# One decoder layer on one core: the sample's value products written to two halves of the PE array, the first chunk in two transfers, and two groups of splits issued earlier

## The chip, the core and the metric

The kernel runs on one core of one Trainium2 chip. The metric is the device time of one execution in microseconds (us), lower is better. The time before is 885.13 us, the median of three executions (884.75 to 885.17). One further execution was recorded by the hardware profiler, and all rows quoted below come from that one.

Names used throughout: PE is TensorE (PEld its weight loads, LDWEIGHTS), DVE is VectorE, ACT is ScalarE, POOL is GpSimd, and SP is the engine that issues most of the DMA transfers. Where an engine's name ends in q, its instruction sequencer is meant.

## The reference

One layer of a decoder is computed for two groups of requests that share the weights: a prompt of 512 tokens, and a sample of 8 requests with 8 new tokens each (64 tokens). The model width is 1024.

```
h   = x @ w_in                      # u | v | q | k | values | gate_A | gate_B
u   = gelu(h_u);  v = layer_norm(gelu(h_v))
y_a = u * (tril(W_s[g]) @ v_chunk + b_s[g])          # 8 groups, chunks of 128 tokens
y_b = attention(q, k, values)       # 16 heads on 4 key/value heads, window 128, sinks, relative bias
m   = (sigmoid(gate_A) * (y_a @ w_pa) + sigmoid(gate_B) * (y_b @ w_pb)) @ w_o
x   = layer_norm(alpha * x + m)
x   = layer_norm(alpha * x + (silu(x @ w_gate) * (x @ w_up)) @ w_down)
```

For the sample, each of the 8 requests attends to 128 cached keys and values and to its own new ones. The outputs are both groups' rows, the updated windows of keys and values, and the normalised v rows of the sample.

## The kernel before

**Precision and splits.** All large products are made in float32 quality from two pieces per operand: `split` (L116) copies a source to a "hi" tile in the fp32r type on ACT (L117) and puts source minus hi in a "lo" tile on DVE (L118). A product is three matmuls: hi by hi, hi by lo, lo by hi (`product` L287, `fm` L300, `tm` L313). Weights arrive as units of 128x1024 in a ring of three raw buffers, and hi and lo live in rings of four each. So a weight unit is fetched by SP, split on ACT and DVE, and read by PE, each some units ahead of the next.

**Order.** The kernel is written against a framework that records the instructions and orders them per engine; where the code says `manual_schedule`, the order is the order in which the code calls them. Every engine runs its own instructions in that order, and semaphores tie the engines together.

**Opening (L400 to L438).** The first products (key tile 0 and query tile 0) run over the 8 chunks of the model width. A chunk holds 576 token columns (512 + 64) and 256 weight columns in one tile, `open{k}`. Chunk 0 comes in three transfers (288 token columns, 256 weight columns, 288 token columns), each other chunk in one of 832 columns. For each chunk ACT and DVE split the tokens into X and the weights into hi and lo, and PE runs 12 matmuls of 288 columns into `ps`. Ahead of that `warm_up` (L392) runs six matmuls of zeros.

**Sample's value products (L733, `sample_values`).** The probabilities of the sample lie transposed in `spT` (cached keys, 128 rows) and `spN` (new keys, 64 rows). For each of the 4 key/value heads g there is one matmul with the new values as weights (64 rows, 64 columns, 256 moving columns) and 8 matmuls, one per request, with the cached values `vc` as weights (128 rows, 64 columns, 32 moving columns). They are in plain float32, and each is two PE instructions in the trace. The result `pso` stands in partitions 0 to 63 of a PSUM bank, for g = 0 and 2 in columns 0 to 255 and for g = 1 and 3 in columns 256 to 511. These 36 matmuls stand between the first and the second weight unit of the first half of the v projection (`acc_v`, L915 to L921).

**Pairs (L216, `pair`).** Two output tiles that share their activations are made with seven half products instead of eight, Strassen-like, of 12 matmuls each. Their weights are B11, B21, B22 and combinations T1 to T4 of them. PE's order in a pair is B11, T1, (the T4 of the pair before), T2, B22, B21, T3. The weights are split in groups: B11 and T1 from buffer a, "B22, B21" from buffer b, "T3, T2" from buffer t (step "2" of `weight_group`, L199), T4 last. `plan` says ahead of which half product each split is called, and `spots` names the places in a pair at which one piece of waiting work (`todo`) is called (`spare`, L211).

**Gates and merge (L997).** Seven pairs make the remaining gates (i = 0 to 6, tiles `xg, yg, zg`). Their `todo` list holds 17 pieces: 5 steps of the last normalisations, the 8 spatial gates, and 4 of the splits of the gated inputs `yA0` to `yA3`; a pair takes two, at its places 0 and 6, and what is left over is called after the last pair (L1034). Then come the products with w_pa (`pspa`, 48 matmuls each, 5 of them in a row), and then four pairs with w_pb (`xp, yp, zp`), each of the first three followed by one more `pspa` product. In the loop over these pairs (L1086) the split "T3, T2" of pair i was called at place 0 of pair i, that is after `end_pairs` and `times` of pair i-1: these two put on DVE the last multiplications of the pair before (L1092) and those of the `pspa` product (L1064).

Of the kernel before, what the change touches and what calls it, by code (L numbers as in the profile page):

```python
# [18 lines left out]
P = 128  # L19
D = 1024  # L20
KC = D // P
NP = 512
NS = 64
NT = NP + NS
HB = NT // 2
NB = NP // P
H = 16
HD = 64
# [51 lines left out]
class Builder:  # L80
# [284 lines left out]
    def build(self):  # L365
        psum = lambda name, bufs: self.tc.tile_pool(
            name=name, bufs=bufs, space=bass.MemoryType.PSUM, reuse_waits="tile")
        with psum("pp0", 3) as self.pp, psum("pb0", 2) as self.pb:
            self.constants()
            self.projections_and_attention()  # L370
        with psum("pb", 8) as self.pb:
            self.sample_first()
            self.gmlp()
            self.merge()
            self.output_projection()
            self.ffn()
            self.ffn_down()
# [22 lines left out]
    def load_x(self):  # L400
        nc = self.nc
        self.open = [self.C([NT + 256], F32, f"open{k}") for k in range(KC)]
        self.open_w = [self.phi.tile([P, 1024], F32R, tag="hi", name=f"hi{i}") for i in range(2)], [
            self.plo.tile([P, 1024], F32R, tag="lo", name=f"lo{i}") for i in range(2)]
        for k, t in enumerate(self.open):
            for s in (slice(0, HB), slice(NT, NT + 256), slice(HB, NT)) if k == 0 else (slice(0, NT + 256),):
                nc.sync.dma_start(out=t[:, s], in_=self.I["open"][:, k, s])
            if k == 3:
                self.bias_lookup()
        self.fetch(2)  # L410

    def opening_chunk(self, k, tiles):

        src = self.open[k]
        w = slice(256 * (k % 4), 256 * (k % 4) + 256)
        wh, wl = (t[k // 4][:, w] for t in self.open_w)
        tokens = lambda t0, t1: self.split(
            self.X[:, k, t0:t1], self.X[:, k, NT + t0 : NT + t1], src[:, t0:t1])
        if k:
            tokens(0, NT)  # L420
        else:
            tokens(0, HB)
        self.split(wh, wl, src[:, NT:])
        if k == 0:
            tokens(HB, NT)
        if k == 5:
            self.bias_copies()
        xh, xl = self.xact(k)
        for b in range(2):
            s = slice(b * HB, (b + 1) * HB)  # L430
            for c in range(2):
                o = tiles[c][:, b, :HB]
                cols = slice(P * c, P * c + P)
                self.mm(o, wh[:, cols], xh[:, s], k == 0, False)
                self.mm(o, wh[:, cols], xl[:, s], False, False)
                self.mm(o, wl[:, cols], xh[:, s], False, k == KC - 1)
        if k == 3:
            self.bias_products()  # L438
# [294 lines left out]
    def sample_values(self, vc, pT, pN):  # L733
        nc = self.nc
        po = [self.bank(f"pso{c}") for c in range(2)]
        outs = [po[g // 2][:HD, 256 * (g % 2) : 256 * (g % 2) + 256].rearrange("p (b q) -> p b q", b=DB)
                for g in range(G)]
        for g, o in enumerate(outs):
            self.mm(o, self.avS[:NS, HD * g : HD * g + HD], pN[:NS, :, 32 * g : 32 * g + 32], True, False)
            for b in range(DB):  # L740
                self.mm(o[:, b], vc[b // 4][:, b % 4, HD * g : HD * g + HD], pT[:, b, 32 * g : 32 * g + 32],
                        False, b == DB - 1)
        for g, o in enumerate(outs):
            for r in range(4):
                i = r % 2
# [7 lines left out]
    def projections_and_attention(self):  # L753
# [4 lines left out]
        self.kraw = misc[:, :384].rearrange("p (c t) -> p c t", c=2)  # L758
        self.Z = self.C([G, 4, 32], F32, "Z")
        self.kt, self.qs, self.u, self.T = [], {}, [], []  # L760
        self.warm_up()
        tiles = [self.PS(f"ps0_{c}") for c in range(2)]
        with self.tc.manual_schedule():
            self.load_x()
# [232 lines left out]
    def merge(self):  # L997
# [27 lines left out]
        with self.tc.manual_schedule():  # L1025
            for i in range(7):
                if i in (3, 4):
                    g, u = (self.SG(f"gb{i}_{k}") for k in range(2))
                else:
                    t = self.C([2, NT], F32, f"T{i}")  # L1030
                    g, u = t[:, 0], t[:, 1]
                (T if i < 3 else gB).extend((g, u))
                gates(i, g, u, i < 6)
        for w in self.todo:  # L1034
            w()
# [50 lines left out]
        def pairs(i):  # L1086
# [27 lines left out]
            else:  # L1114
                late, last = one, one
            stacks = (stack,) if i else ()
            plan = {0: (w["2"],) if i else (), 2: (one,), 3: (w["4"],), 6: (late,) + stacks, 7: (last,) + stacks}
            self.pair(f"p{i}", left, g, u, lambda: mul(ga[:, lo], g[:, lo], ga[:, lo]), final, plan=plan)
            if follows:
                self.w = nxt[0]  # L1120
                f = lambda t: t.rearrange("p (a b) -> p a b", a=KC)
                ps = product(plain + i, tuple(f(t) for t in self.pieces[n]))
                self.end_pairs()
                times(plain + i, ps)

# [311 lines left out]
def _opening(x, w_in):  # L1437

    w = np.concatenate([w_in[:, 3072 : 3072 + P], w_in[:, 2048 : 2048 + P]], 1)
    return np.concatenate([x.T, w], 1).reshape(KC, P, NT + 256).transpose(1, 0, 2)  # L1440


_OUTS = {
# [56 lines left out]
```

## Time and profile before

| What | Value |
|---|---|
| Median of three executions | 885.13 us |
| Profiled execution, its own time | 885.03 us |
| Span from its first to its last instruction | 883.3 us |
| PE busy in the span | 872.7 us (99%) |
| DVE, ACT, POOL busy | 630.2 us, 406.2 us, 193.9 us |
| Mean granted TensorE clock | 0.997 |
| Sample's value products on PE | from 192.03 to 198.51 us |

In a row of the timeline the first number is the start in us from the span's start and the second the duration in us of all instructions that the row merges; then come the engine, the source line, the operation, the names of what is written and read with its shape, and the count. In square brackets stands how long the engine sat idle before, and what ended that. Matmuls are pipelined: each is recorded as longer than the distance to the next, so distances between starts tell the pace.

### The profile page before, as it was taken

What the parts mean: (1) busy time and instruction counts of PE and PEld (TensorE: products, weight loads), DVE (VectorE), ACT (ScalarE), POOL (GpSimd) and SP (SyncE); (2) the same over time, 40 slices, a digit from 0 to 9 for tenths busy, and PEclk for the clock granted to TensorE, in tenths of its full rate; (3) what the DMA queues carried; (4) which work ended last, traced back from release to release, by engine and by line L of the source; (5) the groups of instructions that cost most, each with busy time, mean ns of one, the idle gap of its engine ahead of it and who ended that gap; (6) DMA issues with size and microseconds to landing.
All of it is one profiled execution on the core that took longest, in us unless ns stands there. A gap on an engine that the chain in (4) does not pass through costs nothing.

```text
span 883.3 us, 14728 instructions
## 1 busy us (share of the span) xinstructions
PE 872.7 (99%) x5907; PEld 820.6 (93%) x5907; DVE 630.2 (71%) x933; ACT 406.2 (46%) x770; POOL 193.9 (22%) x205
## 2 busy tenths in 40 slices
PE   9999999999999999999999999999999999999996
PEld 7999999988899999999888999999999998888885
DVE  5878897646789779767768777777777789224237
ACT  6566666565364456233522544444444457111110
POOL 1013324241342113033302222222222210000003
PEclk9999999999999999999999999999999999999998
DMA  8422125145023224324550022322333235222202
GB/s 303 153 99 72 50 72 163 45 170 162 29 104 102 75 93 144 135 78 159 179 187 14 1 72 96 96 96 96 96 97 96 96 96 191 96 72 96 72 1 107
DMA packets 31312, 91.85 MB, mean 104 GB/s; under 512 B 3979, under 2 KB 9516, under 8 KB 31212
## 3 DMA queue, kind: packets, MB, share of 16 engines
q1 hardware_dynamic: 30908, 88.64, 30.1%
q10 hardware_dynamic: 336, 2.28, 0.7%
q8 instruction: 46, 0.75, 0.4%
q14 instruction: 22, 0.18, 0.1%
HBM read 86.77 MB, written 6.10 MB: 105 GB/s over the span
## 4 chain that ended last, share of the span: by engine, by line
PE 93%; DVE 4%; ACT 1%; issue 1%; DMA 0%; POOL 0%; SPq 0%; DVEq 0%; ACTq 0%; POOLq 0%
PE d L298 16%; PE xf L298 14%; PE zf L298 7%; PE acc_v L298 6%; PE acc_o L298 6%; PE pspa L298 6%; PE xg L298 5%; PE psu L298 5%; PE yf L298 4%; PE psq L298 4%; PE ffn L298 3%; PE zg L298 3%; PE xp L298 2%; PE psav L298 2%; PE psg L298 1%; PE ps L298 1%
## 5 line engine op out<-in xcount | busy, mean ns | idle before, releaser
L118 DVE TENSOR_TENSOR lo<-raw,hi 128x1024 fp32r<-128x1024 f32 x70 | 86.2, 1239 | 93.4 <-ACT hi L117 93.0
L118 DVE TENSOR_TENSOR glo<-raw,ghi 128x1024 fp32r<-128x1024 f32 (+1 forms) x93 | 100.8, 1087 | 55.1 <-ACT ghi L117 55.1
L298 PE MATMUL d<-hi,h 128*128 128x512 f32 (+1 forms) x440 | 128.0, 368 | 0.0
L117 ACT CAST hi<-raw 128x1024 fp32r<-128x1024 f32 x70 | 72.7, 1049 | 103.2 <-PE d L298 82.6
L117 ACT CAST ghi<-raw 128x1024 fp32r<-128x1024 f32 (+1 forms) x93 | 83.4, 900 | 59.1 <-DVE raw L180 54.5
L298 PEld LDWEIGHTS d<-hi,h 128*128 128x128 f32 x440 | 79.8, 188 | 13.8
L298 PE MATMUL d<-lo,h 128*128 128x512 f32 (+1 forms) x242 | 89.6, 370 | 0.0
L180 POOL TENSOR_TENSOR raw<-raw,t 128x512 f32<-128x512 f32 x31 | 40.7, 1314 | 197.8 <-DVE glo L118 151.4
L180 POOL TENSOR_TENSOR t<-raw,raw 128x512 f32<-128x512 f32 x31 | 42.2, 1361 | 118.5 <-DVE raw L180 118.5
L298 PE MATMUL xf<-x1T,ghi 128*128 128x288 f32 x320 | 65.0, 295 | 0.0
L118 DVE TENSOR_TENSOR glo<-t,ghi 128x1024 fp32r<-128x1024 f32 x31 | 64.5, 2082 | 0.0
L298 PEld LDWEIGHTS d<-lo,h 128*128 128x128 f32 x242 | 45.6, 188 | 7.8
L298 PEld LDWEIGHTS xf<-x1T,ghi 128*128 128x128 f32 x320 | 51.4, 188 | 0.3 <-DVE u L229 0.2
L328 POOL TENSOR_SCALAR lnr<-lnmv 128x1 f32<-128x1 f32 (+1 forms) x15 | 13.2, 883 | 168.1 <-DVE lnmv L346 164.8
L642 POOL TENSOR_SCALAR_AFFINE_SELECT pc<-pt 128x512 fp32r<-128x512 f32 x24 | 23.2, 968 | 113.4 <-ACT pt L117 111.7
L298 PE MATMUL xf<-x1T,glo 128*128 128x288 f32 x160 | 47.1, 294 | 0.0
L298 PE MATMUL acc_o<-hi,m 128*128 128x512 f32 x144 | 46.3, 391 | 0.0
L298 PE MATMUL pspa<-yA,hi 128*128 128x288 f32 x256 | 44.6, 294 | 0.3 <-DVE yA L118 0.3
L618 ACT ACTIVATE work<-work,att 128x128 f32<-128x128 f32 x64 | 25.0, 392 | 42.1 <-DVE att L615 37.6
L298 PE MATMUL psu<-X,hi 128*128 128x288 f32 x256 | 44.1, 294 | 0.0
L298 PE MATMUL acc_v<-hi,X 128*128 128x512 f32 x128 | 41.6, 391 | 0.0
L298 PE MATMUL psq<-X,hi 128*128 128x288 f32 x224 | 38.8, 294 | 0.3 <-DVE kt L510 0.3
(369 smaller groups left out, 2479.6 us busy)
## 6 DMA issues: line engine op xcount, KB each, us to landing
raw<-in_wall_dram SPq DMA_DIRECT2D x132, 512.0 KB
open<-in_open_dram SPq DMA_DIRECT2D x7, 416.0 KB
xr<-in_xT_dram SPq DMA_DIRECT2D x8, 288.0 KB
z<-in_xtok_dram SPq DMA_DIRECT2D x4, 512.0 KB
out_y_prompt_dram<-z SPq DMA_DIRECT2D x3, 512.0 KB
circ<-bout SPq DMA_DIRECT2D x1, 1024.0 KB
Bsel<-circ SPq DMA_DIRECT2D x2, 512.0 KB
kc<-in_kcT_dram SPq DMA_DIRECT2D x2, 512.0 KB
```

The costliest lines, as they stand in the source:

```text
L117: self.nc.scalar.copy(out=hi, in_=src)
L118: return self.nc.vector.tensor_tensor(out=lo, in0=src, in1=hi.bitcast(F32), op=ALU.subtract)
L180: sub = lambda e, out, x, y: e.tensor_tensor(out=out, in0=x, in1=y, op=ALU.subtract)
L298: self.last_mm = self.nc.tensor.matmul(out, l, r, start=start, stop=stop, **more)
L328: self.nc.gpsimd.tensor_scalar_add(r[:n], mv[:n, 1:2], EPS)
L618: nc.scalar.activation(out=pr[:, r], in_=sel[:, r], func=AF.Exp, bias=nm[:, r : r + 1], accum_out=rs[:, r : r + 1])
L642: self.selected = nc.gpsimd.affine_select(out=f(out[:, i]), in_=f(pt[:, i].bitcast(F32)), pattern=[[0, 4], [sign, P]], compare_op=cmp, fil ...
```

## The change

There are four edits.

1. `sample_values`: key/value heads 1 and 3 now write partitions 64 to 127 of their bank, columns 0 to 255, where heads 0 and 2 write partitions 0 to 63. All four matmuls with the new values come first; then, for each bank, the matmuls of its two heads alternate request by request.
2. Opening: the host puts the weight columns ahead of the token columns in each chunk. Chunk 0 comes in two transfers, of 544 columns (weights and the first 288 tokens) and of 288. `warm_up` is called ahead of `constants`.
3. Pairs with w_pb: step "2" (T3, T2) of the next pair is called right after the `pspa` product and ahead of `end_pairs`.
4. Last pair of the gates (i = 6): `spots` becomes (0, 4, 5, 6), so four pieces of `todo` are called within it.

```diff
         with psum("pp0", 3) as self.pp, psum("pb0", 2) as self.pb:
+            self.warm_up()
             self.constants()
...
-            for s in (slice(0, HB), slice(NT, NT + 256), slice(HB, NT)) if k == 0 else (slice(0, NT + 256),):
+            for s in (slice(0, 256 + HB), slice(256 + HB, 256 + NT)) if k == 0 else (slice(0, 256 + NT),):
                 nc.sync.dma_start(out=t[:, s], in_=self.I["open"][:, k, s])
...
-        src = self.open[k]
+        first, src = self.open[k][:, :256], self.open[k][:, 256:]
...
-        self.split(wh, wl, src[:, NT:])
+        self.split(wh, wl, first)
...
-        outs = [po[g // 2][:HD, 256 * (g % 2) : 256 * (g % 2) + 256].rearrange("p (b q) -> p b q", b=DB)
+        outs = [po[g // 2][HD * (g % 2) : HD * (g % 2) + HD, :256].rearrange("p (b q) -> p b q", b=DB)
                 for g in range(G)]
+        hd, q = (lambda g: slice(HD * g, HD * g + HD)), (lambda g: slice(32 * g, 32 * g + 32))
         for g, o in enumerate(outs):
-            self.mm(o, self.avS[:NS, HD * g : HD * g + HD], pN[:NS, :, 32 * g : 32 * g + 32], True, False)
+            self.mm(o, self.avS[:NS, hd(g)], pN[:NS, :, q(g)], True, False)
+        for c in range(2):
             for b in range(DB):
-                self.mm(o[:, b], vc[b // 4][:, b % 4, HD * g : HD * g + HD], pT[:, b, 32 * g : 32 * g + 32],
-                        False, b == DB - 1)
+                for g in (2 * c, 2 * c + 1):
+                    self.mm(outs[g][:, b], vc[b // 4][:, b % 4, hd(g)], pT[:, b, q(g)],
+                            False, b == DB - 1)
...
-        self.warm_up()
         tiles = [self.PS(f"ps0_{c}") for c in range(2)]
...
                 (T if i < 3 else gB).extend((g, u))
+                if i == 6:
+                    self.spots = (0, 4, 5, 6)
                 gates(i, g, u, i < 6)
...
-            plan = {0: (w["2"],) if i else (), 2: (one,), 3: (w["4"],), 6: (late,) + stacks, 7: (last,) + stacks}
+            plan = {2: (one,), 3: (w["4"],), 6: (late,) + stacks, 7: (last,) + stacks}
...
                 ps = product(plain + i, tuple(f(t) for t in self.pieces[n]))
+                self.w["2"]()
                 self.end_pairs()
                 times(plain + i, ps)
...
-    return np.concatenate([x.T, w], 1).reshape(KC, P, NT + 256).transpose(1, 0, 2)
+    return np.concatenate([w, x.T], 1).reshape(KC, P, NT + 256).transpose(1, 0, 2)
```

How the order of instructions moves is shown at three places; x4 behind a row counts equal instructions that follow each other.

PE at the sample's value products, before (pso0 and pso1 are the two PSUM banks, vc0 and vc1 the cached values of requests 0 to 3 and 4 to 7, misc holds the new values; heads 0 and 1 go to pso0, heads 2 and 3 to pso1):

```order
L298 MATMUL acc_v0_4_2424<-lo22_2237,XS_102 128x512
L298 MATMUL pso0_2459<-spN_2393,misc_103 64x256
L298 MATMUL pso0_2459<-spT_2383,vc0_1972 64x32 x4
L298 MATMUL pso0_2459<-spT_2383,vc1_1973 64x32 x4
L298 MATMUL pso0_2459<-spN_2393,misc_103 64x256
```

and now:

```order
L298 MATMUL acc_v0_4_2423<-lo22_2236,XS_111 128x512
L298 MATMUL pso0_2458<-spN_2392,misc_112 64x256 x2
L298 MATMUL pso1_2459<-spN_2392,misc_112 64x256 x2
L298 MATMUL pso0_2458<-spT_2382,vc0_1971 64x32 x8
L298 MATMUL pso0_2458<-spT_2382,vc1_1972 64x32 x8
L298 MATMUL pso1_2459<-spT_2382,vc0_1971 64x32 x8
L298 MATMUL pso1_2459<-spT_2382,vc1_1972 64x32 x8
L298 MATMUL acc_v0_0_2419<-hi23_2426,X_110 128x512
```

The four matmuls with 64 rows (spN), which stood one ahead of each head's eight, now stand together; in each later row of eight the two heads of a bank alternate. The number of matmuls is the same.

DVE around the boundary from pair 0 to pair 1 with w_pb, before (t52 is the buffer from which T3 and T2 are split; gb3 rows are the last multiplications of pair 0, T1 rows those of the pspa product):

```order
L118 TENSOR_TENSOR glo52_2_4358<-raw53_4284,ghi52_2_4357 128x1024
L1092 TENSOR_TENSOR gb3_0_3297<-xp0_4253,gb3_0_3297 128x288
L1092 TENSOR_TENSOR gb3_1_3298<-pb0_4252,gb3_1_3298 128x576
L1064 TENSOR_TENSOR T1_3021<-pspa5_0_4362,T1_3021 128x288
L1064 TENSOR_TENSOR T1_3021<-pspa5_1_4363,T1_3021 128x288
L118 TENSOR_TENSOR glo52_4_4435<-t52_4336,ghi52_4_4434 128x1024
L118 TENSOR_TENSOR lo54_4469<-raw54_4294,hi54_4468 128x1024
```

and now:

```order
L118 TENSOR_TENSOR glo52_2_4357<-raw53_4283,ghi52_2_4356 128x1024
L118 TENSOR_TENSOR glo52_4_4412<-t52_4335,ghi52_4_4411 128x1024
L1097 TENSOR_TENSOR gb3_0_3296<-xp0_4252,gb3_0_3296 128x288
L1097 TENSOR_TENSOR gb3_1_3297<-pb0_4251,gb3_1_3297 128x576
L1069 TENSOR_TENSOR T1_3020<-pspa5_0_4361,T1_3020 128x288
L1069 TENSOR_TENSOR T1_3020<-pspa5_1_4362,T1_3020 128x288
L118 TENSOR_TENSOR lo54_4468<-raw54_4293,hi54_4467 128x1024
```

The lo piece of T3 and T2 went ahead of four multiplications. The same holds at the two later boundaries (t55 and t58).

DVE at the end of the last pair of the gates, before (T6 rows are the pair's own additions, hi44/lo44 to hi46/lo46 the weights of the first three pspa products):

```order
L118 TENSOR_TENSOR yA6_3894<-u6_2095,yA6_3894 128x576
L118 TENSOR_TENSOR yA7_3897<-u6_2095,yA7_3897 128x576
L229 TENSOR_TENSOR T6_3731<-zg6_3734,T6_3731 128x288
L229 TENSOR_TENSOR T6_3731<-yg6_3733,T6_3731 128x288
L118 TENSOR_TENSOR yA0_3838<-u0_911,yA0_3838 128x576
L118 TENSOR_TENSOR lo45_3842<-raw45_3656,hi45_3841 128x1024
L229 TENSOR_TENSOR T6_3731<-xg6_3732,T6_3731 128x288
L118 TENSOR_TENSOR lo46_3861<-raw46_3772,hi46_3860 128x1024
L118 TENSOR_TENSOR yA1_3865<-u0_911,yA1_3865 128x576
L118 TENSOR_TENSOR yA2_3868<-u2_1663,yA2_3868 128x576
L118 TENSOR_TENSOR yA3_3871<-u2_1663,yA3_3871 128x576
```

and now:

```order
L118 TENSOR_TENSOR yA6_3893<-u6_2094,yA6_3893 128x576
L118 TENSOR_TENSOR yA0_3810<-u0_910,yA0_3810 128x576
L229 TENSOR_TENSOR T6_3730<-zg6_3733,T6_3730 128x288
L118 TENSOR_TENSOR yA1_3826<-u0_910,yA1_3826 128x576
L229 TENSOR_TENSOR T6_3730<-yg6_3732,T6_3730 128x288
L118 TENSOR_TENSOR yA7_3896<-u6_2094,yA7_3896 128x576
L118 TENSOR_TENSOR yA2_3843<-u2_1662,yA2_3843 128x576
L118 TENSOR_TENSOR lo45_3847<-raw45_3655,hi45_3846 128x1024
L229 TENSOR_TENSOR T6_3730<-xg6_3731,T6_3730 128x288
L118 TENSOR_TENSOR lo46_3866<-raw46_3771,hi46_3865 128x1024
L118 TENSOR_TENSOR yA3_3870<-u2_1662,yA3_3870 128x576
```

yA0 and yA1 moved ahead of the pair's additions from zg and yg, yA2 ahead of lo45, and yA7 behind the addition from yg; yA3 stays behind lo46.

## The prediction

> **What bounds the kernel now.** I read the page's busy shares and its chain of waits first, then what PE's weight loads waited for, then the timeline at the places found there.
>
> ```profile
> span 883.3 us, 14728 instructions
> PE 872.7 (99%) x5907; PEld 820.6 (93%) x5907; DVE 630.2 (71%) x933; ACT 406.2 (46%) x770; POOL 193.9 (22%) x205
> PE 93%; DVE 4%; ACT 1%; issue 1%; DMA 0%; POOL 0%; SPq 0%; DVEq 0%; ACTq 0%; POOLq 0%
> ```
>
> PE is busy for 872.7 of 883.3 us and carries 93% of the chain. So time is only to be had where PE works slowly or stands still, and what is saved there reaches the end as long as nothing further on waits for another engine. The profiled execution took 885.03 us, 0.1 under the median of 885.13; the sum below is made against 885.03. The weight loads show stops more sharply than the matmuls, whose ends are modelled (engine, line, releaser; total us, times, longest):
>
> ```profile
> PEld pso L298 <- issue: 1.9, 5, 0.4
> PEld ps L298 <- ACT hi L117: 1.5, 2, 0.8
> PEld xp L298 <- DVE glo L118: 1.1, 3, 0.4
> PEld pspa L298 <- DVE yA L118: 0.5, 1, 0.5
> ```
>
> The four edits stand at these four rows: sample's values (pso), opening (ps), T2 (xp), gated inputs (pspa).
>
> **Edit 1, sample's values.** PE's timeline at head 0 and behind head 3, then the weight loads, then the group of the spN matmuls (min/median/max ns):
>
> ```profile
> 192.03 0.64 PE L298 MATMUL pso<-spN,misc 64*64 64x256 f32 x2
> 192.60 1.12 PE L298 MATMUL pso<-spT,vc 128*64 128x32 f32 x16
> 193.65 0.64 PE L298 MATMUL pso<-spN,misc 64*64 64x256 f32 x2
> ...
> 198.51 0.50 PE L298 MATMUL acc_v<-hi,X 128*128 128x512 f32 x1
> ```
> ```profile
> 192.60 1.01 PEld L298 LDWEIGHTS pso<-spT,vc 128*64 128x64 f32 x16 [0.39 <-issue]
> ```
> ```profile
> L298 PE MATMUL pso<-spN,misc x8: 376/402/427, 192.0 to 197.2; 64*64 64x256 f32 x8
> ```
>
> One head takes 192.03 to 193.65, 1.62 us: 0.57 until its spT matmuls start, and 1.05 for these 16 (66 ns each, the run-out included). Four heads are 6.48 us, which is 192.03 to 198.51. All use half the array's columns. The spN pair lasts 0.64 with a median of 0.40 for one, so the second starts 0.24 after the first.
>
> Now eight spN instructions come first: 0.57 + 6 x 0.24 = 2.01 us if the halves take turns, 0.57 + 2 x 0.24 = 1.05 if they run side by side. The 64 spT instructions: 4 x 1.05 = 4.20 in turn, 2.10 side by side. So the block is 6.21 or 3.15 us, and the gain 0.3 or 3.3. The 0.39 idle ahead of the spT loads comes once instead of four times; that is inside these numbers. Which end holds is read from the kernel's one other use of parts of the array, the sample's scores, where 64 instructions go to eight parts (two halves of the rows, four quarters of the columns):
>
> ```profile
> L298 PE MATMUL pss<-kc,Z x64: 275/276/301, 167.9 to 168.8; 64*32 64x136 f32 x64
> ```
> ```profile
> 167.93 1.20 PE L298 MATMUL pss<-kc,Z 64*32 64x136 f32 x64
> 169.06 0.40 PE L298 MATMUL psg<-X,hi 128*128 128x288 f32 x1
> ```
>
> They take 1.13 us, 18 ns each. At spN's pace (0.24 us for 256 columns) one of 136 columns needs 0.13 alone: 64 in one row would be 8.2 us, and with only the two row halves side by side 4.1. So column parts do run side by side, weight loads included. I take 3.15 us: **gain 3.3** (0.3 to 3.6, the upper end if the run-outs fall to one as well).
>
> A rule speaks against this. The Trainium skill (TensorE: Matmul & The Clock Gate, Part 3: Packing small matmuls) says that a weight load overlaps with matmuls in flight only where the row group differs; the two halves here share all rows. By it the block would stay near 6.21 us. The score row, with four column parts to each row half, disagrees with it; it remains as a rival below. Another page (TensorEngine Tiling (Array Packing), Key Properties) lets different tiles load and multiply in parallel, as that row does.
>
> **Edit 3, T2.** ACT, DVE and PE at the first of three boundaries between pairs:
>
> ```profile
> 379.68 1.22 DVE L118 TENSOR_TENSOR glo<-raw,ghi 128x1024 fp32r<-128x1024 f32 x1
> 381.66 1.05 ACT L117 CAST ghi<-t 128x1024 fp32r<-128x1024 f32 x1 [2.58 <-PE pspa L298]
> 383.45 0.46 DVE L1092 TENSOR_TENSOR gb<-xp,gb 128x288 f32<-128x288 f32 x1 [2.56 <-PE xp L298]
> 384.49 0.81 DVE L1064 TENSOR_TENSOR T<-pspa,T 128x288 f32<-128x288 f32 x2
> 385.22 1.73 DVE L118 TENSOR_TENSOR glo<-t,ghi 128x1024 fp32r<-128x1024 f32 x1
> ...
> 386.43 0.43 PE L298 MATMUL xp<-SA,ghi 128*128 128x288 f32 x2
> 387.00 0.40 PE L298 MATMUL xp<-SA,glo 128*128 128x288 f32 x1
> 387.24 0.30 PE L298 MATMUL xp<-SA,ghi 128*128 128x288 f32 x1
> 388.09 1.23 DVE L118 TENSOR_TENSOR lo<-raw,hi 128x1024 fp32r<-128x1024 f32 x1 [1.14 <-ACT hi L117]
> ```
>
> DVE is idle from 380.90 to 383.45 waiting for PE's last product of the pair, while the hi piece is there at 382.71; only the order keeps glo<-t behind the multiplications. PE needs it at 386.69 (two matmuls at the 0.13 pace after 386.43), gets it at 387.00, and the next matmul follows after 0.24 instead of 0.13: 0.31 + 0.10 = 0.41 us lost. The wait list has three such stops: **gain 1.2**. In the new order glo<-t runs from 382.71 to 383.94 (at 1.23 unshared), 2.7 us ahead of its need. ACT's hi copy can't start earlier than 381.66, since its buffer is freed by pspa, but that is enough. Late instead are the four multiplications, by 0.5 us, done at about 385.8; POOL's additions and a PSUM bank follow them, and DVE itself is next wanted at 388.09, where it had been idle for 1.14. So nothing on the path pays. Without that cover the price would be 0.5 us a boundary, 1.5 in all: bounds 1.2 gained, 0.3 lost.
>
> **Edit 4, gated inputs.** PE, ACT and DVE behind the last gate pair:
>
> ```profile
> 331.43 0.29 PE L298 MATMUL xg<-X,glo 128*128 128x288 f32 x1
> 331.71 0.53 PE L298 MATMUL pspa<-yA,hi 128*128 128x288 f32 x2
> 332.51 0.53 PE L298 MATMUL pspa<-yA,hi 128*128 128x288 f32 x2 [0.27 <-DVE yA L118]
> 332.87 0.42 PE L298 MATMUL pspa<-yA,lo 128*128 128x288 f32 x2
> ```
> ```profile
> 331.00 0.66 ACT L117 CAST yA<-u 128x576 fp32r<-128x576 f32 x1
> 331.57 1.99 ACT L117 CAST hi<-raw 128x1024 fp32r<-128x1024 f32 x2
> ```
> ```profile
> 335.28 2.09 DVE L118 TENSOR_TENSOR yA<-u,yA 128x576 fp32r<-128x576 f32 x3
> ```
>
> The matmul at 332.87 is the fifth after 331.43 and was due at 332.09: 0.78 lost, as yA0 is split only at 331.00. Now yA0 and yA1 are split before it (DVE done by 330.2), and the 331.00 slot is yA2's, needed from 333.15. The next candidate is yA3: it stands behind two weight copies on ACT and behind lo46 on DVE, so its lo piece ends near 336.0, where the first of the three yA ended before; PE asks for it behind the pair's last 12 matmuls, near 336.0 as well. I leave 0.1 for that: **gain 0.7** (0.3 to 0.8).
>
> **Edit 2, opening.** ACT's casts, PE's start on chunk 1, and two stretches (us; busy of PE, PEld, DVE, ACT, POOL; clock; DMA share; GB/s):
>
> ```profile
> 3.08 0.43 ACT L117 CAST X<-open 128x288 fp32r<-128x288 f32 x1 [0.81 <-DMA open<-in_open_dram]
> ...
> 6.03 0.67 ACT L117 CAST X<-open 128x576 fp32r<-128x576 f32 x1 [0.94 <-DMA open<-in_open_dram]
> 7.06 0.89 PE L298 MATMUL ps<-X,hi 128*128 128x288 f32 x2 [0.49 <-ACT hi L117]
> ```
> ```profile
> 3.10:4.40 1.30, 1.30 (x5) 0.50 (x4) 0.79 (x2) 0.76 (x2) 0.00 (x0) 1.00 0.99 201
> 4.40:6.00 1.60, 1.51 (x9) 1.21 (x9) 0.46 (x1) 0.43 (x1) 0.00 (x0) 1.00 0.98 358
> ```
>
> PE's steady run begins with chunk 1, whose landing releases ACT at 6.03. In the early stretch the DMA engines are busy (0.99) yet move 201 GB/s, with the pieces of chunk 0; with the full rows of the later chunks it is 358. Two transfers instead of three make fewer and longer rows: moving chunk 0's 426 KB takes 2.1 us at 201, 1.2 at 358. A third of the rows goes, so I take a third to half of that 0.9: **gain 0.4**. Bounds: nothing, if chunk 1 lands when it did; 0.55. The first cast, at 3.08, may come up to 0.4 later, as it waits for 278 KB instead of 147. That delays the first six matmuls of chunk 0, and PE stands idle for 0.49 ahead of chunk 1, which covers it; uncovered it would be a loss of 0.4. The order of `warm_up` is worth nothing: PE idles behind it anyway.
>
> **Sum.** 3.3 + 1.2 + 0.7 + 0.4 = 5.6 us. 885.03 - 5.6 = 879.4; with the 0.1 between that execution and the median, **879.5**.
>
> **Rivals.**
> *Halves in turn.* The block stays at 6.21: total gain 0.3 + 1.2 + 0.7 + 0.4 = 2.6, **882.5**. For it: all spT loads use the same rows, and at 66 ns for 32 moving columns something other than the columns sets the pace. Against it: the score rows at 18 ns. 13%.
>
> *The time comes back in the v projection.* With edits 1 and 2 PE is 3.7 us ahead at its second half, which has little cover:
>
> ```profile
> 217.68 0.39 PE L298 MATMUL acc_v<-hi,X 128*128 128x512 f32 x1
> ```
> ```profile
> 220.08 1.22 DVE L118 TENSOR_TENSOR lo<-raw,hi 128x1024 fp32r<-128x1024 f32 x1
> ```
>
> The last weight unit's lo is ready at 221.30 and needed by the 20th matmul after 217.68, at 0.23 each, 222.0. If DVE's work there did not move with PE, PE would wait 3.7 - 0.7 = 3.0 us: **882.5**. Against it: this split waits for a buffer that PE itself frees, and the input sums ahead of it on DVE wait for PE's last reading of spN, which now comes earlier. 5%.
>
> *Slower: each change of half empties the array.* Heads alternate, 31 changes. If each cost the 0.39 idle seen ahead of the spT loads, the block would be 6.21 + 12.1 = 18.3, a loss of 11.8, less 2.3 from the other edits: **894.6**. It decides from 2.6 / 31 = 0.08 us a change. Against it: the score matmuls change parts too, at 18 ns. 3%.
>
> *Edits do less than they say.* Halves in turn, and the opening or T2 uncovered as bounded above: gains of 0.7 to 1.8, **about 884**. 4%.
>
> **Chances and range.** My forecast has 75%, with its own range 878.8 to 880.6 from the bounds of the terms. The rivals at 882.5 hold 18% and are mostly taken in: 878.8 to 882.8. A difference under 0.2% (1.8 us) can't be told from none in this kernel. Faster: the forecast, most of the two at 882.5, 0.90. Same: 0.06. Slower: 0.04.
>
> **What would show it.** Right: the pso block about 3.2 us long, with spT instructions near 33 ns apart; no xp stop by glo at the three boundaries; pspa's stop gone or near 0.1; chunk 1's PE start near 6.65. Wrong: a block over 5 us, a new stop of acc_v by DVE near 218, or multiplications of the pairs showing up as releasers of PE.

## The result and the profile after

The changed kernel takes 880.61 us in the median (879.99 to 881.21, 4 runs), the kernel before, run beside it, 885.15 us (884.75 to 885.52, 4 runs). The ratio is 0.9949 with a 95% interval of 0.9931 to 0.9966: faster by 4.5 us, or 0.5%. One of the twelve executions of the kernel with edit 2 alone, at a granted clock of 0.82, took 978 us and is in none of the times and ratios below. The forecast of 879.5 is 1.1 us too low; the range 878.8 to 882.8 holds the time, while the forecast's own narrower range, 878.8 to 880.6, ends just below it. The profiled execution after took 881.21 us, the highest of its four, so its span shrinks by 3.8 us only (883.3 to 879.5).

The page of the changed kernel, then the first rows of what its weight loads waited for (us in total, times, longest):

```profile
span 879.5 us, 14727 instructions
PE 867.8 (99%) x5907; PEld 818.0 (93%) x5907; DVE 628.4 (71%) x933; ACT 405.2 (46%) x770; POOL 190.1 (22%) x205
PE 93%; DVE 4%; ACT 1%; DMA 1%; issue 0%; POOL 0%; DVEq 0%; SPq 0%; ACTq 0%; POOLq 0%
```
```profile
PEld ps L298 <- ACT hi L117: 2.8, 2, 1.5
PEld L298 <- DVE ones L385: 1.2, 1, 1.2
PEld acc_v L298 <- DVE lo L118: 1.2, 1, 1.2
PEld L298 <- issue: 1.1, 4, 0.3
PEld pso L298 <- issue: 0.7, 2, 0.4
```

PE still bounds the kernel. The three xp stops by glo and the pspa stop are gone from the list, and pso has 0.7 us of idle time where it had 1.9. But ps waits 2.8 us in place of 1.5, and there is a stop that the kernel before did not have: acc_v, 1.2 us for a lo piece. Both kernels' PE rows at five places tell what each stretch gained or lost. Before (its row behind pso, at 198.51, stands in the prediction):

```profile
12.59 0.72 PE L298 MATMUL bias<-bsel 33*128 33x272 f32 x2
...
243.07 0.42 PE L298 MATMUL xg<-X,ghi 128*128 128x288 f32 x2
...
365.80 0.42 PE L298 MATMUL xp<-Y,ghi 128*128 128x288 f32 x2
...
424.14 0.42 PE L298 MATMUL zp<-SB,ghi 128*128 128x288 f32 x2
```

And after:

```profile
13.29 0.72 PE L298 MATMUL bias<-bsel 33*128 33x272 f32 x2
...
192.73 1.08 PE L298 MATMUL pso<-spN,misc 64*64 64x256 f32 x8
193.74 2.06 PE L298 MATMUL pso<-spT,vc 128*64 128x32 f32 x64
195.73 0.50 PE L298 MATMUL acc_v<-hi,X 128*128 128x512 f32 x1
...
241.40 0.42 PE L298 MATMUL xg<-X,ghi 128*128 128x288 f32 x2
...
363.31 0.42 PE L298 MATMUL xp<-Y,ghi 128*128 128x288 f32 x2
...
420.40 0.42 PE L298 MATMUL zp<-SB,ghi 128*128 128x288 f32 x2
```

| stretch of PE up to | before | after | shift so far | of this stretch | forecast |
|---|---|---|---|---|---|
| bias products (opening) | 12.59 | 13.29 | +0.70 | +0.70 | -0.4 |
| acc_v behind the pso block | 198.51 | 195.73 | -2.78 | -3.48 | -3.3 |
| first gate pair (v projection) | 243.07 | 241.40 | -1.67 | +1.11 | 0 |
| first merge pair (gated inputs) | 365.80 | 363.31 | -2.49 | -0.82 | -0.7 |
| behind the last T2 boundary | 424.14 | 420.40 | -3.74 | -1.25 | -1.2 |

Three of the four edits came within 0.2 us of their price. What is missing is 1.1 us at the opening, where a gain became a loss, and 1.1 us given back in the v projection.

**The opening after**: ACT's casts and PE's start on chunk 1, then two stretches (us; busy of PE, PEld, DVE, ACT, POOL; clock; DMA share; GB/s).

```profile
3.62 0.43 ACT L117 CAST X<-open 128x288 fp32r<-128x288 f32 x1 [1.35 <-DMA open<-in_open_dram]
...
4.27 0.43 ACT L117 CAST X<-open 128x288 fp32r<-128x288 f32 x1
6.72 0.67 ACT L117 CAST X<-open 128x576 fp32r<-128x576 f32 x1 [2.03 <-DMA open<-in_open_dram]
...
7.75 0.89 PE L298 MATMUL ps<-X,hi 128*128 128x288 f32 x2 [1.23 <-ACT hi L117]
```
```profile
3.10:4.40 1.30, 0.88 (x3) 0.00 (x0) 0.32 (x1) 0.78 (x3) 0.00 (x0) 1.00 1.02 347
4.40:6.00 1.60, 1.59 (x10) 1.49 (x11) 0.85 (x3) 0.29 (x1) 0.00 (x0) 1.00 0.92 260
```

Chunk 0 is complete earlier, as the forecast had it: its second half is cast at 4.27, not 4.65, and the early stretch moves 347 GB/s in place of 201. Chunk 1 nevertheless comes at 6.72 in place of 6.03: from 4.40 to 6.00 the rate is 260 GB/s where it was 358.

**The v projection after**: SP's issue of the last xr pair, POOL's first use of it, ACT's copy and DVE's split of the last weight unit, and PE's load that waits for it. Of before, only the first two are new; its split, at 220.08, is in the prediction; the last row is its weight load that corresponds to the waiting one.

```profile
207.95 0.33 SPq L963 DMA_DIRECT2D xr<-in_xT_dram  x1
212.34 0.81 POOL L960 TENSOR_TENSOR s<-xr 128x288 f32<-128x288 f32 x1 [6.15 <-DMA xr<-in_xT_dram]
216.74 1.06 ACT L117 CAST hi<-raw 128x1024 fp32r<-128x1024 f32 x1
218.92 1.22 DVE L118 TENSOR_TENSOR lo<-raw,hi 128x1024 fp32r<-128x1024 f32 x1
220.18 0.19 PEld L298 LDWEIGHTS acc_v<-lo,X 128*128 128x128 f32 x1 [1.22 <-DVE lo L118]
```
```profile
210.25 0.33 SPq L960 DMA_DIRECT2D xr<-in_xT_dram  x1
...
213.24 1.08 POOL L957 TENSOR_TENSOR s<-xr 128x288 f32<-128x288 f32 x1 [4.75 <-DMA xr<-in_xT_dram]
...
221.76 0.19 PEld L298 LDWEIGHTS acc_v<-lo,X 128*128 128x128 f32 x1
```

PE is 2.78 us earlier here and the xr transfer is issued 2.3 earlier, but POOL gets it only 0.9 earlier: 4.39 us behind its issue in place of 2.99. All that follows on POOL, ACT and DVE hangs on that landing, up to the lo split, which is 1.16 earlier. The prediction's slack of 0.7 is the time until a matmul; the load that reads the piece starts at 221.76 in the kernel before, 0.46 behind the end of the split at 221.30. 2.78 less 1.16 less 0.46 is 1.16: the stop is 1.2 long in the list, and 1.11 by PE's rows.

### The profile page after: what moved, and what is told of

It reads as the page before. It is cut to its first block, busy times and chain, and to the rows that moved or that the text cites. A ratio compares the mean times of both kernels' runs of the same rounds, so it can differ in the third digit from the quotient of the medians.

```text
span 879.5 us, 14727 instructions
## 1 busy us (share of the span) xinstructions
PE 867.8 (99%) x5907; PEld 818.0 (93%) x5907; DVE 628.4 (71%) x933; ACT 405.2 (46%) x770; POOL 190.1 (22%) x205
## 3 DMA queue, kind: packets, MB, share of 16 engines
q10 hardware_dynamic: 336, 2.28, 0.7%
## 4 chain that ended last, share of the span: by engine, by line
PE 93%; DVE 4%; ACT 1%; DMA 1%; issue 0%; POOL 0%; DVEq 0%; SPq 0%; ACTq 0%; POOLq 0%
PE d L298 16%; PE xf L298 15%; PE zf L298 7%; PE acc_o L298 6%; PE pspa L298 6%; PE xg L298 5%; PE psu L298 5%; PE acc_v L298 5%; PE yf L298 4%; PE psq L298 4%; PE ffn L298 3%; PE xp L298 3%; PE zg L298 3%; PE psav L298 2%; PE psg L298 1%; PE zp L298 1%
```

## Experiments

The theory: each edit is worth what its place shows, edit 2 costs time by itself, and the stop at acc_v comes from the late landing of the last xr pair, which shares the DMA engines with weight prefetches that now stand close ahead of it (the raw tiles 29 and 30 of 512 KB each, issued 4.2 and 2.4 us earlier; in the kernel before raw 29 was 8.7 us ahead). The rivals: the opening's loss is chance; the stop comes from the order on ACT and DVE alone; edit 1 gains by its order and not by the halves.

**The halves** (h_turns). Only the order of the spT instructions changes, so that neighbours stand on the same half:

```diff
         for c in range(2):
             for b in range(DB):
-                for g in (2 * c, 2 * c + 1):
+                for g in (c, c + 2):
                     self.mm(outs[g][:, b], vc[b // 4][:, b % 4, hd(g)], pT[:, b, q(g)],
```

> The changed kernel with only the order of the 64 spT instructions altered: heads 0 and 2 alternate (both on the lower half of the columns), then heads 1 and 3 (both on the upper half). Theory A, the gain comes from neighbours on different halves running side by side: spT falls back from 31 to about 66 ns each, 4.2 us for 64, and the pso block from 3.0 to 5.1 us. Rival B, it is the order of the work that gains (the spN first, no idle time between heads, another bank for each neighbour): the block stays near 3.0. With A the v projection's stop of 1.2 us goes too, since PE comes there 2.1 us later, so that the time rises by 0.9 only, to 881.5.

PE's rows of this run:

```profile
193.70 3.71 PE L298 MATMUL pso<-spT,vc 128*64 128x32 f32 x64
197.35 0.50 PE L298 MATMUL acc_v<-hi,X 128*128 128x512 f32 x1
```

The 64 take 3.65 us (193.70 to 197.35), 57 ns each, where they took 1.99, 31 ns, in the changed kernel; the block is 4.66 long in place of 3.00. So neighbours on different halves do run side by side, and that is worth 1.66. The starts of the single instructions in the traces say the same: in the changed kernel two start 7 ns apart and the next two 59 ns behind them, in this run one starts every 58 ns, but for a few in the middle, where the heads change from one half to the other. In the kernel before it is 58 ns too within a head, so the other bank, which neighbours have here and had not there, gains nothing.

Neither theory had the rest: the block is still 1.82 shorter than the 6.48 before. The spT part falls from 4 x 1.05 = 4.20 to 3.65, mainly because idle time and run-outs come once and not four times. The spN part falls from 4 x 0.57 = 2.28 to 1.01, but this is not free of the halves: its order is that of the changed kernel, where heads 0 to 3 alternate halves, and its eight instructions start in four pairs 7 ns apart, where before the second of a head came 0.27 behind the first. No run has the eight spN in a row on one half. One run took 882.48 us, 1.0 above expectation: the stop at acc_v is still there (0.8), as the xr pair too is issued 1.0 later, at 208.99, than in the changed kernel.

**Edit 1 alone** (e_values), in the kernel before, with `sample_values` as in the change and nothing else:

> The kernel before with edit 1 alone (sample's values on two halves). Theory A, the losses are tied to their places: the pso block is 3.0 us (6.48 before), and the v projection's last lo split, set by the landing of the input sums' last xr transfers, moves less than PE, so acc_v waits for DVE about 1.1 us as in the changed kernel; net gain 3.5 - 1.1 = 2.4 us, 882.8. Rival B, the stop at acc_v came with the later opening of the changed kernel (DVE work there did not shift with PE by those 0.7): then it is longer here, 1.9, and the gain 1.6, 883.6. Rival C, the stop belongs to other edits: no stop, 881.7.

882.26 us (881.51 to 882.43, 5 runs), ratio 0.9960 (0.9947 to 0.9974): a gain of 3.2 beside 885.48 for before. The block is 3.00 us here as well (192.31 to 195.31), and the weight loads' list has

```profile
PEld acc_v L298 <- DVE lo L118: 0.8, 1, 0.8
```

So the stop comes with edit 1 and needs neither the later opening nor another edit; A is right in kind, 0.3 us off in the stop and 0.5 in the time.

**Edits 3 and 4 alone** (e_t2gates), in the kernel before:

```diff
+                if i == 6:
+                    self.spots = (0, 4, 5, 6)
                 gates(i, g, u, i < 6)
...
-            plan = {0: (w["2"],) if i else (), 2: (one,), 3: (w["4"],), 6: (late,) + stacks, 7: (last,) + stacks}
+            plan = {2: (one,), 3: (w["4"],), 6: (late,) + stacks, 7: (last,) + stacks}
...
+                self.w["2"]()
                 self.end_pairs()
                 times(plain + i, ps)
```

> The kernel before with edits 3 and 4 alone (T2's and the gated inputs' splits). Theory A, each is worth what its own place shows: three xp stops of 0.42 and the pspa stop of 0.8 go, 2.1 us together, 883.3. Rival B, these gains hung on PE being earlier from the other edits: under 1.5 us, above 883.9.

882.96 us (882.53 to 883.77, 7 runs) beside 885.20, ratio 0.9974 (0.9963 to 0.9984): a gain of 2.2. Its span is 2.1 shorter than that of before (883.3 to 881.2), and none of the four stops is left. The two terms stand by themselves.

**The opening.** First the changed kernel with edit 2 taken back (u_open), then the kernel before with edit 2 alone (e_open). What is put in or taken out is the same in both:

```diff
+            self.warm_up()
             self.constants()
...
-            for s in (slice(0, HB), slice(NT, NT + 256), slice(HB, NT)) if k == 0 else (slice(0, NT + 256),):
+            for s in (slice(0, 256 + HB), slice(256 + HB, 256 + NT)) if k == 0 else (slice(0, 256 + NT),):
...
-    return np.concatenate([x.T, w], 1).reshape(KC, P, NT + 256).transpose(1, 0, 2)
+    return np.concatenate([w, x.T], 1).reshape(KC, P, NT + 256).transpose(1, 0, 2)
```

> The changed kernel with edit 2 undone (three transfers for chunk 0, warm-up where it was). Theory A, the two larger transfers themselves cost the 0.7 us seen at the opening: chunk 1's first matmul comes back from 7.75 to about 7.06 and everything behind it shifts by 0.7, 879.9. Rival B, the 0.7 is how the transfers happened to run in that one execution: the time stays at 880.6, and chunk 1 starts anywhere between 7.0 and 7.8. Rival C, the edit gains 0.4 as predicted, hidden in that execution: 881.0.

> The kernel before with edit 2 alone (chunk 0 in two transfers, warm-up first). Theory A, the edit costs time by itself: the first cast comes at 3.6 to 3.8 in place of 3.0 to 3.1, chunk 1 lands no earlier than 6.0 and in some executions up to 0.7 later, so that the bias products come at 12.5 to 13.3 in place of 12.4 to 12.7: a loss of 0 to 0.7, 885.6 in the median. Rival B, the forecast's reading: 0.4 gained, 884.8.

Without edit 2: 879.93 us (879.72 to 880.40, 5 runs), ratio 0.9938 (0.9925 to 0.9950). Edit 2 alone: 885.38 (884.93 to 886.33, 11 runs) beside 885.25, ratio 1.0001 (0.9992 to 1.0010). The times alone tell no loss from none, and the interval of the second run leaves room for a gain of 0.4; that both medians go the other way speaks against one. The traces say more, since every run here has one opening or the other:

| opening | run | first cast | chunk 1 cast | bias products |
|---|---|---|---|---|
| three transfers | before | 3.08 | 6.03 | 12.59 |
| | e_values | 3.02 | 6.04 | 12.62 |
| | u_open | 3.04 | 5.97 | 12.54 |
| | e_t2gates | 3.01 | 6.12 | 12.68 |
| | best | 3.02 | 5.85 | 12.42 |
| two transfers | after | 3.62 | 6.72 | 13.29 |
| | f_xr | 3.68 | 5.98 | 12.54 |
| | f_lo | 3.76 | 6.11 | 12.98 |
| | h_turns | 3.69 | 6.26 | 12.99 |
| | e_open | 3.68 | 6.29 | 13.06 |

(Left out are the two runs below that change the opening further.) With two transfers the bias products come at 13.0 in the middle, with three at 12.6, and with two never earlier than 12.54. The 0.7 of the profiled execution was near the high end; the usual loss is 0.4, and f_xr shows none. Chunk 1 lands no earlier for the rows saved in chunk 0: its cast starts at 5.98 to 6.72 with two transfers and at 5.85 to 6.12 with three. The lower rate behind chunk 0 is seen in other executions too; the first row is from u_open, with three transfers, the second from f_lo, with two:

```profile
4.40:6.00 1.60, 1.30 (x7) 0.86 (x7) 0.46 (x1) 0.47 (x2) 0.00 (x0) 1.00 1.03 377
```
```profile
4.40:6.00 1.60, 1.45 (x6) 1.43 (x7) 0.99 (x3) 0.43 (x2) 0.00 (x0) 1.00 0.88 283
```

377 GB/s against 283; in this stretch the six executions with three transfers have 356 to 390, the six with two 260 to 316. Added up from the rates of three stretches, 1.14 to 1.19 MB are moved from 1.80 to 6.00 us with three transfers and 1.14 to 1.23 MB with two: the merged transfer moves its bytes earlier, but by the time chunk 1 lands hardly more has been moved. Why the rate falls behind it was not settled.

**One more warm-up matmul** (w_warm). In f_lo chunk 1 was there at 6.11, and still the bias products came 0.4 later than in f_xr. PE's rows of f_lo show another loss, three matmuls in 0.72 us, 0.24 each, where the pace is 0.13:

```profile
5.48 0.68 PE L298 MATMUL ps<-X,hi 128*128 128x288 f32 x2
5.96 0.44 PE L298 MATMUL ps<-X,lo 128*128 128x288 f32 x1
6.20 0.68 PE L298 MATMUL ps<-X,hi 128*128 128x288 f32 x2
```

This lasts until 8.4 in f_lo, and about as long in h_turns and e_open. In the five executions with three transfers it ends by 6.5 at the latest. With two, PE stands idle for 0.43 to 0.56 us between warm-up and chunk 0, since the first cast is later. So the changed kernel was run with that idle time filled:

```diff
-        for _ in range(6):
+        for _ in range(7):
             self.mm(ps, z[:, :P], z[:], True, True)
```

> The changed kernel with seven warm-up matmuls in place of six, so that PE has work from 1.24 until about 4.4 us, where the first cast chunk is ready, in place of standing idle for 0.43 to 0.56. Theory A, that idle time is why PE still ran at half pace (0.24 us a matmul) until 8.2 to 8.4 in two of four runs of this opening: with it filled PE is at full pace (0.13) by 6.6 at the latest, as with the opening before, and the bias products come at 12.5 to 12.7 if chunk 1 lands at 6.0 to 6.1; 880.3. Rival B, the moment of full pace has nothing to do with that idle time and falls anywhere between 4.4 and 8.4: then it can lie behind 6.6 here too, and the time stays at 880.6.

880.78 us (880.56 to 880.89, 4 runs), ratio 0.9947 (0.9934 to 0.9960): no change. In its trace PE is at full pace from 5.4, which fits A, but the bias products come at 13.38, since here chunk 2 landed late, at 8.32 where it was 7.93 in the changed kernel:

```profile
5.41 0.51 PE L298 MATMUL ps<-X,hi 128*128 128x288 f32 x2
```
```profile
8.32 0.67 ACT L117 CAST X<-open 128x576 fp32r<-128x576 f32 x1 [1.14 <-DMA open<-in_open_dram]
```

One execution can't settle whether the idle time causes the half pace. It does show that the landing alone can cost as much.

**The stop at acc_v: the transfer** (f_xr). In the changed kernel, the prefetch of raw 30 is queued behind the last xr pair:

```diff
-        us = [self.unit(2, ahead=int(n < 3)) for n in range(4)]
+        us = []
+        for n in range(4):
+            with self.tc.issue_after(self.xr_last.ins) if n == 1 else nullcontext():
+                us.append(self.unit(2, ahead=int(n < 3)))
```

> The changed kernel with one weight prefetch (raw30) queued behind the last two xr transfers in place of ahead of them. Theory A, the xr landing sets the last lo split in the v projection, and it is late because 512 KB of raw share the DMA engines with it: xr3 and xr7 land at least 1.2 us earlier, the lo split too, acc_v's wait falls from 1.2 to 0.2 or less, 879.5. Rival B, the order on DVE and ACT alone holds the split (statistics and a subtraction stand ahead of it): wait and time stay, 880.6.

880.55 us (880.06 to 880.87, 5 runs), ratio 0.9943 (0.9931 to 0.9956): no change, and the stop is 1.3. But the transfer did what A says. The same rows as above, in this run:

```profile
207.52 0.33 SPq L966 DMA_DIRECT2D xr<-in_xT_dram  x1
210.50 0.81 POOL L963 TENSOR_TENSOR s<-xr 128x288 f32<-128x288 f32 x1 [4.74 <-DMA xr<-in_xT_dram]
212.25 0.43 ACT L117 CAST XS1h<-xr 128x288 fp32r<-128x288 f32 x1 [3.22 <-POOL xr L963]
212.70 1.28 ACT L908 ACT_TABLE_LOAD   x1
218.34 1.22 DVE L118 TENSOR_TENSOR lo<-raw,hi 128x1024 fp32r<-128x1024 f32 x1
```

POOL has xr 2.98 us behind its issue, 1.4 sooner than in the changed kernel. The scheduler, though, answered the new order with another on ACT: the XS1h cast now stands ahead of the table load and the first gelu, which had run while ACT waited for xr. The lo split follows POOL by 7.84 us instead of 6.58, and 1.26 of the 1.4 is gone. PE also comes 0.7 us earlier here, since its opening had no loss (12.54 in the table above), so the stop is as long as before.

**The stop at acc_v: the order** (f_lo). In the changed kernel, the statistics are put behind the last split on DVE:

```diff
+        us = [self.unit(2, ahead=int(n < 3)) for n in range(4)]
         for t in range(NB + 1):
-            evacuate(t, acc[t], 0)
+            with self.tc.issue_after(self.last_split.ins):
+                evacuate(t, acc[t], 0)
...
-        us = [self.unit(2, ahead=int(n < 3)) for n in range(4)]
```

> The changed kernel with the last weight unit's lo split put ahead of the layer norm's statistics on DVE; ACT's order and all transfers stay. Theory A: the hi copy still ends near 217.80, since ACT waits for xr; lo then runs 217.8 to 219.0 in place of 218.92 to 220.14, and acc_v's wait falls from 1.2 to about 0.1, 879.5. Rival B, the statistics come later and hold the normalization and what PE needs next: the time comes back there, 880.6 or more.

880.60 us (879.74 to 880.68, 5 runs), ratio 0.9941 (0.9929 to 0.9954): no change; the stop is 0.9. ACT, DVE and POOL there:

```profile
216.50 1.06 ACT L117 CAST hi<-raw 128x1024 fp32r<-128x1024 f32 x1
```
```profile
217.59 1.98 DVE L118 TENSOR_TENSOR lo<-raw,hi 128x1024 fp32r<-128x1024 f32 x1 [0.48 <-ACT hi L117]
```
```profile
217.20 1.29 POOL L180 TENSOR_TENSOR t<-raw,raw 128x512 f32<-128x512 f32 x1 [3.50 <-DVE raw L180]
```

The split starts 1.33 earlier, near the expected 217.8, but lasts 1.98 in place of 1.22. The weight pair's subtractions on DVE had slipped ahead of it and released POOL's, which runs beside the split until 218.49.

**Both causes taken away, with the opening before** (best). The prefetch behind xr; the hi copy ahead of the gelus on ACT; the lo split ahead of the statistics; the pair's subtractions behind it; three transfers for chunk 0:

```diff
+        for t in range(NB + 1):
+            with ExitStack() as s:
+                if t:
+                    s.enter_context(self.tc.issue_after(self.last_cast.ins))
+                    s.enter_context(self.tc.issue_after(self.last_split.ins))
+                evacuate(t, acc[t], 0)
...
-        self.first_pair()
+        with self.tc.issue_after(self.behind.ins):
+            self.first_pair()
```

> Edits 1, 3 and 4 with the opening of before; one weight prefetch queued behind the last two xr transfers; the last weight unit's hi copy put ahead of the gelus on ACT, and its lo split ahead of the statistics on DVE, with the pair's subtractions behind it. Theory A, the wait at acc_v is made of the late xr landing and of the work put ahead of the split: with both gone there is no wait (1.2 in the changed kernel, 0.3 to 0.9 in others), 879.3. Rival B, the later gelus and statistics hold up the next bank or the normalization and the time comes back behind it: 879.9 or more.

879.41 us (879.24 to 880.10, 5 runs), ratio 0.9936 (0.9922 to 0.9949), and no acc_v row in the list of waits:

```profile
209.57 1.11 POOL L968 TENSOR_TENSOR s<-xr 128x288 f32<-128x288 f32 x1 [4.71 <-DMA xr<-in_xT_dram]
```
```profile
215.46 1.23 DVE L118 TENSOR_TENSOR lo<-raw,hi 128x1024 fp32r<-128x1024 f32 x1 [0.17 <-ACT hi L117]
```

The split is done at 216.69, and no other wait has taken the place of the stop. The span, 877.5, is 2.0 under that of the changed kernel. The fair comparison is u_open, which has the same opening: 0.5 in the span and in the median (879.93), with runs that overlap, so that the rows show that the stop is gone and the times alone do not. Over all executions the stop follows the landing and the order (xr pair issued; POOL's first use behind that; lo split behind POOL; stop); in the first three, without edit 1, PE is not ahead there:

| run | raw 30 | issued | POOL | lo split | stop |
|---|---|---|---|---|---|
| before | 2.9 us ahead | 210.25 | +2.99 | +6.84 | none |
| e_t2gates | 2.9 us ahead | 210.38 | +2.93 | +6.91 | none |
| e_open | 3.1 us ahead | 210.90 | +2.87 | +6.75 | none |
| after | 2.4 us ahead | 207.95 | +4.39 | +6.58 | 1.2 |
| e_values | 2.4 us ahead | 207.17 | +4.29 | +6.60 | 0.8 |
| w_warm | 2.4 us ahead | 207.70 | +3.98 | +6.60 | 0.4 |
| u_open | 2.4 us ahead | 207.63 | +3.21 | +6.61 | 0.3 |
| h_turns | 2.4 us ahead | 208.99 | +4.48 | +6.61 | 0.8 |
| f_lo | 2.4 us ahead | 207.89 | +4.19 | +5.51 | 0.9 |
| f_xr | behind | 207.52 | +2.98 | +7.84 | 1.3 |
| best | behind | 206.61 | +2.96 | +5.89 | none |
| best2 (below) | behind | 207.09 | +3.28 | +5.62 | none |

u_open differs from the changed kernel in the opening alone, and its stop of 0.3 in place of 1.2 is the landing's: with the same order of transfers the landing varies from one execution to the next, here from +3.21 to +4.48.

**Chunk 1 in two halves** (best2). The kernel of the run before, with

```diff
-        if k:
+        if k > 1:
             tokens(0, NT)
...
-        if k == 0:
+        if k < 2:
             tokens(HB, NT)
```

> As the run before, and chunk 1 of the opening cast in two halves of the tokens around its weights, as chunk 0 is. Theory A, PE's steady run begins when the first half of X and the weights of chunk 1 are cast: 0.43 + 0.40 in place of 0.67 + 0.40 us behind its landing, so PE starts chunk 1 at about 6.8 in place of 7.05, 879.05. Rival B, the extra casts make chunk 2 late on ACT, or the first lo pieces hold PE: nothing gained, 879.3.

879.19 us (878.75 to 879.55, 5 runs), ratio 0.9931 (0.9918 to 0.9943): the lowest median of all, 6.0 under before, but not told apart from the run before it. PE starts 0.79 us behind chunk 1's landing (6.14 to 6.93), in place of 1.03 (5.85 to 6.88), as A says; chunk 1 landed 0.3 later in this execution, so the trace shows no end that is earlier.

## Why the prediction was right, and where not

**Edit 1**, 3.3 forecast, 3.48 measured: right, term by term. Side by side the spN were to take 1.05 and the spT 2.10; they take 1.01 and 1.99. The score row, whose column parts ran at 18 ns, was the right row to trust. The rule of the Trainium skill (TensorE: Matmul & The Clock Gate, Part 3: Packing small matmuls), by which a weight load overlaps with matmuls in flight only where the row group differs, does not hold here: 64 instructions that share all rows and alternate halves go at 31 ns, those on one half at 57. The step that was off is the price of the halves in turn: "66 ns each, the run-out included" was used for 16 where for 64 in a row it is 57, so that the spT part of "6.21" should have been 3.65 and not 4.20. With the forecast's 2.01 for the spN, which no run has in turn in one row, the block would be 5.66, and the rival priced at 882.5 would have come near 882 (an estimate).

**Edit 3**, 1.2 forecast, 1.25 measured: right in each step. DVE's rows at the first boundary (2.5 us earlier than before on the clock of the trace):

```profile
380.26 1.23 DVE L118 TENSOR_TENSOR glo<-t,ghi 128x1024 fp32r<-128x1024 f32 x1 [1.70 <-ACT ghi L117]
...
382.43 0.82 DVE L1069 TENSOR_TENSOR T<-pspa,T 128x288 f32<-128x288 f32 x2
```

glo<-t starts at 380.26, or 382.75 in the time of before, where the forecast had 382.71; the multiplications end at 383.25, or 385.74, forecast 385.8. Nobody waits for them.

**Edit 4**, 0.7 forecast, 0.82 measured: right; the 0.1 left for yA3 did not occur. Its lo piece is done at 334.37, and PE goes on with it at 334.35 without idle time (the two ends differ by what the profile resolves):

```profile
333.62 0.75 DVE L118 TENSOR_TENSOR yA<-u,yA 128x576 fp32r<-128x576 f32 x1
```
```profile
334.35 0.61 PE L298 MATMUL pspa<-yA,hi 128*128 128x288 f32 x3
```

**Edit 2**, 0.4 gained forecast, 0.7 lost in the profiled execution, some 0.4 in most: wrong in sign. The step that failed is "a third of the rows goes, so I take a third to half of that 0.9". It took for granted that time saved on chunk 0's transfer is passed on to chunk 1's landing. Chunk 0 was complete 0.2 to 0.7 sooner, chunk 1 was not. PE's idle time ahead of chunk 1 was to hide the later first cast. In f_xr it did, but in three of five executions matmuls at half pace used it up, and in the profiled one chunk 1 itself was late. The usual loss equals the 0.4 that the prediction named as the price without cover, but not for the reason named: the first cast came some 0.66 later, not up to 0.4, and what cost the time was the half pace or the late chunk.

**The v projection.** The rival that time comes back there had 5%, and it happened in part, 1.11 us of the 3.0 priced; "a new stop of acc_v by DVE near 218", which the prediction named as a sign of being wrong, came beside the signs of being right. The step that failed is the argument against it: "this split waits for a buffer that PE itself frees, and the input sums ahead of it on DVE wait for PE's last reading of spN". They did wait for that, but the last column's sums waited longer for a transfer, whose releaser stood in the POOL rows of the kernel before and was not taken into account. The slack against it was 0.46 and not 0.7, as worked out above. What this rival was missing, on the other side, is that the transfer's issue does follow PE (2.3 of 2.78); only its landing doesn't.

By its own terms: 5.6 forecast, less 1.1 at the opening and 1.1 in the v projection, and 0.3 more from edits 1, 3 and 4, is the 3.8 of the two spans, within 0.1. The medians differ by 4.5, since the profiled execution after was the slowest of its four; among all executions here its bias products and its stop are near the late end too. So the time lies in the range because the largest term held, and near the edge of the forecast's own range because the two losses added up. That range can't be worked out again "from the bounds of the terms": the upper bounds, 3.6, 1.2, 0.8 and 0.55, end at 879.0 and not 878.8.

## What to carry to other kernels

When PE is moved ahead by microseconds, follow every input of the next stage back to its transfer and not to the engine that splits it: here a load that had one more prefetch close ahead of it was there up to 1.5 us later behind its issue. A transfer that was merged to save rows delayed the first use of its first piece by 0.5 to 0.8 us in every execution here, and brought the next transfer in no earlier; look first whether the trace shows that this one waits for it. Small matmuls on half of the columns went at 31 ns in place of 57 where neighbours in the order stood on different halves; taking idle time and run-outs between groups of them away was worth some 0.5 us more.

## Hardware behaviour that was not expected

PE ran the opening's matmuls at 0.24 us in place of 0.13 until between 4.6 and 8.6 us into the program, differing from one execution to the next, while the profile's granted clock says 1.00 in these stretches (the rows of f_lo above). The Trainium skill (TensorE: Matmul & The Clock Gate, Part 1: The HAM clock gate) says that full speed comes after a busy window of about 3.4 us that runs freely, so that its moment varies between runs. The half pace agrees, and so does that the moment varies; the spread here, some 4 us, is wider than the 500 ns to either side that the section gives for matmuls back to back.

A DVE subtraction that started while a POOL subtraction was running took 1.98 us in place of 1.22 (f_lo). It ended 1.08 behind POOL's end, and so did, within 0.01, two later ones: at 420.40 in the changed kernel (2.13 us, POOL busy until 421.45) and at 419.77 in f_lo (1.81 us, POOL busy until 420.49). The Trainium skill (SBUF — State Buffer, SBUF: two separate sides) says that VectorE with two SBUF inputs and GpSimd share a pair of ports as an exclusive lock, so that the one who comes second is blocked for the other's whole instruction; with POOL's end at 218.49 and 1.22 us of work the split would end at 219.71, and it ended at 219.57, so the two agree to 0.14.

The first of the last two xr transfers (288 KB each) was used 2.9 to 3.3 us behind its issue where one prefetch of 512 KB had been issued in the 4.2 us ahead of it (before, e_t2gates, e_open, f_xr, best, best2), and 3.2 to 4.5 us behind it where two had been (the other six). The two groups overlap slightly, with 3.28 in the first and 3.21 in the second.
